# Delta stage: the output gates' projections dealt over the stage and kept in DRAM, the values beside the blockwise inverses

## The chip, the cores and the metric

One core of a Trainium2 chip. The metric is device time in microseconds. The core's engines are named as in the profile: PE is TensorE (PEld its weight loads), DVE is VectorE, ACT is ScalarE, POOL is GpSimd, SP is the engine that issues most DMAs. Each engine runs its own instructions in order and waits for the others on semaphores.

## The reference, cut to what matters

The program is a mixer with a layer of experts, a banded attention and, last, a gated delta rule over 256 tokens and 16 meta tokens (`L` = 272, width 1024). Only the last part, the delta stage, is touched:

```
def deltanet_mixer(h, norm_w, w_in, conv_w, a_log, dt_bias, o_norm_w, w_out):
    u = rms_norm(h, norm_w) @ w_in
    qkv, z, b, a = jnp.split(u, ...)
    qkv = jax.nn.silu(causal_depthwise_conv(qkv, conv_w))
    q, k, v = ...                       # 8 heads of q and k, 16 of v, 128 wide
    o = chunked_gated_delta_rule(q, k, v, beta, g)
    o = rms_norm(o, o_norm_w) * jax.nn.silu(z)
    return o.reshape(B, L, DN_VALUE_WIDTH) @ w_out
...
def step(S, inp):                       # one chunk of the delta rule
    m = strictly_lower(kb @ kc.T * decay)
    sol = triangular_solve(m + eye, rhs)
    u, w = sol[..., :DN_HEAD_DIM_V], sol[..., DN_HEAD_DIM_V:]
    v_new = u - w @ S
    o = (qc * exp(gcum)) @ S + attn @ v_new
    S = S * exp(g_last) + k_state.T @ v_new
```

The gate is `silu(z)`. It is first needed when the outputs `o` are scaled, at the very end; it depends on nothing but the normalised input `h` and 16 blocks of the weights.

## The kernel before

All products are fp32 split in two parts, `hi` and `lo`, and take three matmuls. The work comes in units (`unit`, L269): SP loads a 512 KB block of weights `raw`, ScalarE rounds it to `hi`, VectorE takes the residual `lo` (L274), and TensorE runs 24 matmuls (L284, L285, L286 in turn, the third with `lo`) into a PSUM bank `pj_ps`, of which there are two. The ring of weights has four `raw`, three `hi` and three `lo`. `proj_t` and `proj` are the functions; the delta stage has 49 units: one for the decays (`ba`), 8 for k, 8 for q (260 columns), 16 for v (272 columns), 16 for the gates z (256 columns).

A keys' unit is scaled by the norm's `R` on its way out of PSUM (`cpad`, L1324), since the normalised input isn't there yet; later ones use the normalised `nh`, `nl` and are evicted by ScalarE (`cpad` L1327, `craw` or `qT` L1328). VectorE runs the causal convolution (L1339), four taps each.

Behind the keys come the products `kk`, their norms (`kkd` L1409 and L1410), `lbeta`, sixteen exponentials on ScalarE (L1392, `hh<-dec`), and the matrices `U` (L1483), in two halves. These are stored to DRAM (`e<-U`, L1486) and loaded in another layout (`ab<-e`, L1505), 128 matrices of 32x32, each on one partition. VectorE inverts them by substitution in 31 steps of two operations (`subst`: `sb_t` L1236, `ub` L1238). The result goes through DRAM again (`e<-ub`, `U<-e`), and 8 groups of four heads are put together by small matmuls (`r`, `zt`, `z`, L1533 to L1559): the blockwise inverse.

The substitution and the blockwise inverse are a generator, `inverse()`. The main line is another, `values()`, and whenever it yields, `next(side, None)` issues a piece of the inverse: three steps (`SR` = 3), or a third of a group. The scheduler puts each engine's instructions in its own order, by its own model of their times; `issue_after` pins an instruction behind another.

In the main line stand the 8 units of q, the 16 of v with their norms, transposes and products `attend`, then the gates of heads 0 to 7 (8 units, in `gates`, kept in SBUF as `z`). Then the recurrence runs by groups of four heads (`first(h0)`), where `first(8)` and `first(12)` each run four more gates ahead of their step. The out projection (`w_o`, 16 units of 512 columns) is last.

Of the kernel before, what the change touches and what calls it, by code (L numbers as in the profile page):

```python
# [6 lines left out]
F32 = mybir.dt.float32  # L7
# [10 lines left out]
T = 256  # L18
M = 16
L = M + T  # L20
# [170 lines left out]
class Net:  # L191
    def __init__(self, nc, tc, ap, cat, dat, dump):
        self.nc, self.tc, self.ap, self.dump = nc, tc, ap, dump
        self.cat, self.dat = cat, dat
        self.open = []

    def pool(self, name, bufs=1, space=None, side=None):
        kw = {}
# [69 lines left out]
    def unit(self, src, eng=None):  # L268
        nc = self.nc  # L269
        raw = self.fetch(src)  # L270
        hi = self.ring.tile([128, 1024], F32R, name="hi", bufs=3)
        lo = self.ring.tile([128, 1024], F32R, name="lo", bufs=3)
        nc.scalar.activation(hi, raw, AF.Copy)  # L273
        self.residual = (eng or nc.vector).tensor_sub(lo, raw, hi).ins  # L274
        return hi, lo

    def split(self, hi, lo, src):
# [947 lines left out]
    def subst(self, u, a, n, work, eng):  # L1225

        nc = self.nc
        p = a.shape[0]
        nc.gpsimd.memset(u, 0.0)
        diag = bass.AP(tensor=u.tensor, offset=u.offset, ap=[list(u.ap[0]), [n + 1, n]])  # L1230
        nc.gpsimd.memset(diag, 1.0)
        for s in range(n - 1):
            r = n - 1 - s
            t = work.tile([128, 256], F32, name="sb_t", bufs=1)[:p, :(s + 1) * r]
            t = t.rearrange("p (j c) -> p j c", c=r)
            eng.tensor_tensor(t, u[:, 0:s + 1, s:s + 1].to_broadcast([p, s + 1, r]),  # L1236
                              a[:, s, None, s + 1:].to_broadcast([p, s + 1, r]), op=ALU.mult)
            eng.tensor_sub(u[:, 0:s + 1, s + 1:], u[:, 0:s + 1, s + 1:], t)  # L1238
            yield

    def delta(self, NZ=2, AH=4, KN=8, SS=1, SR=3, SW=3):
        nc, ap = self.nc, self.ap
        ident, tri = self.c("ident"), self.c("tri")
        conv = self.d("conv").rearrange("p (b i) -> p b i", i=4)
# [1 line left out]
        A = self.pool("deA", side="right")  # L1246
# [7 lines left out]
        (hh, hl), R = self.hT, self.R  # L1254
        V = self.pool("deV", side="right")
        W = self.pool("deW1", side="right")
        units = iter(range(49))
        CH = (slice(0, M), slice(M, M + 128), slice(M + 128, L))


# [4 lines left out]
        def normalise(k):  # L1265
            t = W.tile([128, L], F32, name="nt", bufs=2)
            nc.vector.tensor_mul(t, h4[:, k], R)
            self.split_scaled(nh[:, k], nl[:, k], t, gd[:, k:k + 1])

        def proj(ts=slice(0, L)):  # L1270
            ps = pj.tile([128, 512], F32, name="pj_ps", tag="pj")
            n = ts.stop - ts.start
            u = next(units)
            a = (hh, hl) if u <= KN else (nh, nl)
            self.proj_t(ps[:, :n], self.unit(ap["w_t3"][u]), (a[0][:, :, ts], a[1][:, :, ts]))
            return ps[:, :n]


        X = Slices(V.tile([128, 2048], F32, name="early", tag="8"))
        bt = X.tile([128, L], F32, name="bat")  # L1280
        nc.vector.tensor_mul(bt, proj(), R)
        tp = bank(pb, "tp")
        for c in (1, 2, 0):
            nc.tensor.transpose(tp[:CH[c].stop - CH[c].start, c], bt[:, CH[c]], ident)
# [30 lines left out]
        def conv_head(dst, b, t0=0):  # L1315

            n = L - t0
            t = max(t0 - 4, 0)
            w = [conv[:, b, i:i + 1] for i in range(4)]
            ps = proj(slice(t, L))  # L1320
            src = W.tile([128, L], F32, name="cpad", bufs=2)[:, :L - t]
            early = 8 <= b < 8 + KN
            if early:
                nc.vector.tensor_mul(src, ps, R)  # L1324
                ps = src
            else:
                nc.scalar.activation(src, ps, AF.Copy)  # L1327
            nc.scalar.activation(dst, ps[:, t0 - t:t0 - t + n], AF.Copy, scale=w[3])  # L1328
            for i in (2, 1, 0):

                o = max(3 - i - t0, 0)
                at = t0 - t - 3 + i + o
                x, y = src[:, at:at + n - o], dst[:, o:]
                if early and i == 2:
                    x2 = W.tile([128, L], F32, name="ctap", bufs=2)[:, :n - o]
                    nc.scalar.activation(x2, x, AF.Copy, scale=w[i])
                    nc.gpsimd.tensor_add(y, y, x2)
                else:
                    nc.vector.scalar_tensor_tensor(y, x, w[i], y, op0=ALU.mult, op1=ALU.add)  # L1339
# [72 lines left out]
        def norms(c, p):  # L1412
# [6 lines left out]
            if c < 2:  # L1419
                nc.vector.tensor_tensor(bw[:p, c], bw[:p, c], lb[:p, c], op=ALU.add)  # L1420
                nc.scalar.activation(bw[:p, c], bw[:p, c], AF.Exp)

        for j in range(8):
            conv_head(kT[:, j], 8 + j)
            normalise(j)
            if j == 2:
                cumulate()
            if j in (3, 5, 7):
                silu(kT[:, (0 if j == 3 else j - 1):j + 1])
# [74 lines left out]
        def inverse():  # L1504
            nc.sync.dma_start(ab, e1.rearrange("k b m s c -> (k b m) s c"))  # L1505
            ub = V.tile([128, 32, 32], F32, name="ub", tag="4b")
            for s, _ in enumerate(self.subst(ub, ab, 32, V, nc.vector)):
                if s % SR == SR - 1:
                    yield
            nc.sync.dma_start(e2.rearrange("k b m s c -> (k b m) s c"), ub)  # L1510
            for c in range(2):
                for b, s in enumerate(blocks):
# [56 lines left out]
        def values():  # L1569
            for j in range(8):  # L1570
                conv_head(qT[:, j], j, M)
            v.extend(half("v", c) for c in range(2))
            for h0 in range(0, 16, 4):
                hs = slice(h0, h0 + 4)
                raw = A.tile([128, 4, L], F32, name="craw", bufs=2)
                for j in range(4):
                    conv_head(raw[:, j], 16 + h0 + j)
                    if h0 and j % 2:
                        attend(j // 2, h0 - 4)
                    yield  # L1580
                silu(qT[:, h0 // 2:h0 // 2 + 2], silu(raw))
                for c in range(2):
                    tp = bank(pb, "tp")
                    for j in range(4):
                        nc.tensor.transpose(tp[:, j], raw[:, j, CH[c + 1]], ident)
                    for j in range(0, 4, 2):
                        nc.scalar.activation(v[c][:, h0 + j:h0 + j + 2], tp[:, j:j + 2], AF.Copy,
                                             scale=ri[:, c + 1, (h0 + j) // 2:(h0 + j) // 2 + 1])
                tp = bank(pb, "tp")
                for j in range(4):  # L1590
                    nc.tensor.transpose(tp[:M, j], raw[:, j, CH[0]], ident)
                va = W.tile([M, 4, 128], F32, name="va")
                nc.scalar.activation(va, tp[:M], AF.Copy)
                tp = bank(pb, "tp")
                for j in range(2):
                    nc.tensor.transpose(tp[:M, j], kT[:, h0 // 2 + j, CH[0]], ident)
                ka = W.tile([M, 2, 128], F32, name="ka")
                nc.scalar.activation(ka, tp[:M, 0:2], AF.Copy)
                ps = bank(pb, "mv")
                for j in range(4):  # L1600
                    nc.tensor.matmul(ps[:M, j], um[:, h0 + j], va[:, j], start=True, stop=True,
                                     skip_group_check=True)
                vs = W.tile([M, 4, 128], F32, name="vsA")
                nc.vector.tensor_tensor(vs, ps[:M], bw[:M, 0, hs, None].to_broadcast([M, 4, 128]), op=ALU.mult)
                ps = bank(pb, "mS")
                for j in range(2):
                    nc.tensor.matmul(flat(ps[:, 2 * j:2 * j + 2]), ka[:, j],
                                     flat(vs[:, 2 * j:2 * j + 2]), start=True, stop=True, skip_group_check=True)
                nc.scalar.activation(S[:, hs], ps, AF.Copy)
            for c in range(2):  # L1610
                attend(c, 12)
                yield
            for h0 in range(0, 4 * NZ, 4):
                z = A.tile([128, 4, T], F32, name="z", tag="craw", bufs=2)
                yield from gates(z)
                sz.append(z)
            self.logexp()

        def gates(z):
            for j in range(4):  # L1620
                silu(z[:, j], src=proj(slice(M, L)))
                yield

        sz = []
        done = []
        side = inverse()
        for _ in values():
# [2 lines left out]


        W = self.pool("deW3", side="right")
        onw = self.d("onw")


# [77 lines left out]
        def first(h0):  # L1713
            while (int(h0 >= AH), (h0 - AH) % 16) not in done:
                next(side)
            if h0 >= 4 * NZ:
                z = W.tile([128, 4, T], F32, name=f"z{h0}")
                for _ in gates(z):
                    pass
                sz.append(z)  # L1720
            yield from step(0, h0)

        staged((first(h0) for h0 in range(0, 16, 4)), lambda: [next(side, None) for _ in range(SS)])
# [76 lines left out]
```

## Time and profile before

| | |
|---|---|
| median of 3 runs | 1470.29 us (1468.67 to 1470.91) |
| the profiled execution | 1471.06 us, span 1469.3 us |
| delta stage in the span | from about 1165 us to the end |
| TensorE busy, whole span | 1441.3 us |
| VectorE busy, whole span | 1066.4 us |
| ScalarE busy, whole span | 794.1 us |
| mean granted clock of TensorE | 0.997 |

The span is the time from the first to the last instruction of one profiled execution; 1.8 us lie outside it. Busy times come from the page, and the stage's start from the times of its first matmuls. A row of the trace in time has start, length, engine, line and operation, what is written from what, and in brackets how long the engine stood idle before it and what ended that.

### The profile page before, as it was taken

The numbers are of one execution on the slowest core, as the hardware profiler recorded it, in microseconds if no ns is written. First come the engines' busy times: TensorE is split into PE (matmuls) and PEld (weight loads), VectorE is DVE, ScalarE is ACT, GpSimd is POOL, SyncE is SP. The second block draws the span as 40 slices with busy tenths as digits, with TensorE's granted clock in tenths as the row PEclk, the third lists the DMA queues.
The fourth block names the chain that finished last, engine by engine and source line by source line (L and its number), as shares of the span: only waits on it lengthen the run. The fifth ranks groups of instructions, "written<-read, shape, count | busy, mean of one in ns | idle before, by whom it ended". The sixth has DMA issues, their size and how long they took to land.

```text
span 1469.3 us, 27077 instructions
## 1 busy us (share of the span) xinstructions
PE 1441.3 (98%) x10627; PEld 1323.1 (90%) x10627; DVE 1066.4 (73%) x2127; ACT 794.1 (54%) x1367; POOL 73.8 (5%) x106
## 2 busy tenths in 40 slices
PE   9999999999999999999999999999999989999998
PEld 9889999999999999999888888888898989899777
DVE  7667578789948888898555555555776788895566
ACT  5556545545544444444444445444686667664464
POOL 0000000000000000000000000000113024000020
PEclk9999999999999999999999999999999999999999
DMA  7453364555665545545666666666442444545113
GB/s 244 128 163 93 115 207 143 173 172 161 199 179 161 163 150 168 159 155 168 196 189 198 191 195 197 195 192 192 152 117 85 145 120 129 170 124 158 36 43 115
DMA packets 72223, 229.19 MB, mean 156 GB/s; under 512 B 16048, under 2 KB 16464, under 8 KB 72096
## 3 DMA queue, kind: packets, MB, share of 16 engines
q1 hardware_dynamic: 71408, 225.69, 50.5%
q8 instruction: 83, 1.36, 0.4%
q0 software_dynamic: 400, 1.46, 0.3%
q10 hardware_dynamic: 288, 0.33, 0.1%
q14 instruction: 44, 0.36, 0.1%
HBM read 225.31 MB, written 2.13 MB: 155 GB/s over the span
## 4 chain that ended last, share of the span: by engine, by line
PE 93%; ACT 3%; DVE 2%; issue 1%; DMA 0%; SPq 0%; POOL 0%; ACTq 0%; DVEq 0%
PE pu_ps L284 10%; PE pu_ps L285 9%; PE pu_ps L286 9%; PE acc L284 8%; PE acc L285 8%; PE acc L286 8%; PE pj_ps L284 8%; PE pj_ps L285 8%; PE pj_ps L286 8%; PE pt_ps L912 2%; PE tr_ps L370 1%; PE out L284 1%; PE out L285 1%; PE out L286 1%; ACT hi L273 1%
## 5 line engine op out<-in xcount | busy, mean ns | idle before, releaser
L273 ACT ACTIVATE hi<-raw 128x1024 fp32r<-128x1024 f32 x421 | 444.7, 1058 | 433.8 <-PE pu_ps L285 165.8
L274 DVE TENSOR_TENSOR lo<-raw,hi 128x1024 fp32r<-128x1024 f32 x421 | 516.4, 1228 | 197.1 <-ACT hi L273 195.6
L284 PE MATMUL pu_ps<-x2h,hi 128*128 128x256 f32 x1152 | 330.8, 288 | 0.1
L285 PE MATMUL pu_ps<-x2l,hi 128*128 128x256 f32 x1152 | 326.4, 284 | 0.2 <-DVE x2l L279 0.2
L286 PE MATMUL pu_ps<-x2h,lo 128*128 128x256 f32 x1152 | 326.0, 283 | 0.2 <-DVE lo L274 0.2
L285 PEld LDWEIGHTS pu_ps<-x2l,hi 128*128 128x128 f32 x1152 | 220.9, 192 | 0.4 <-DVE x2l L279 0.4
L286 PEld LDWEIGHTS pu_ps<-x2h,lo 128*128 128x128 f32 x1152 | 220.7, 192 | 0.4 <-DVE lo L274 0.4
L284 PEld LDWEIGHTS pu_ps<-x2h,hi 128*128 128x128 f32 x1152 | 220.5, 192 | 0.3 <-ACT x2h L278 0.3
L285 PE MATMUL acc<-lo,ch 128*128 128x512 f32 x512 | 198.8, 389 | 0.0
L286 PE MATMUL acc<-hi,cl 128*128 128x512 f32 x512 | 198.2, 389 | 0.0
L284 PE MATMUL acc<-hi,ch 128*128 128x512 f32 x512 | 139.0, 389 | 0.0
L284 PE MATMUL pj_ps<-hh,hi 128*128 128x272 f32 (+1 forms) x424 | 123.4, 295 | 4.2 <-DVE cpad L1324 2.6
L285 PE MATMUL pj_ps<-hl,hi 128*128 128x272 f32 (+1 forms) x424 | 123.8, 293 | 0.7 <-DVE hl L330 0.6
L286 PE MATMUL pj_ps<-hh,lo 128*128 128x272 f32 (+1 forms) x424 | 123.7, 293 | 0.0
L286 PEld LDWEIGHTS acc<-hi,cl 128*128 128x128 f32 x512 | 96.1, 188 | 20.0
L285 PEld LDWEIGHTS acc<-lo,ch 128*128 128x128 f32 x512 | 96.1, 188 | 19.8
L284 PEld LDWEIGHTS acc<-hi,ch 128*128 128x128 f32 x512 | 96.0, 188 | 19.9
L284 PE MATMUL pj_ps<-nh,hi 128*128 128x256 f32 (+2 forms) x320 | 93.5, 292 | 2.2 <-ACT craw L1328 2.1
L285 PE MATMUL pj_ps<-nl,hi 128*128 128x256 f32 (+2 forms) x320 | 92.8, 290 | 0.0
L286 PE MATMUL pj_ps<-nh,lo 128*128 128x256 f32 (+2 forms) x320 | 92.1, 288 | 0.0
L284 PEld LDWEIGHTS pj_ps<-hh,hi 128*128 128x128 f32 x424 | 80.1, 190 | 5.9 <-issue 2.9
L285 PEld LDWEIGHTS pj_ps<-hl,hi 128*128 128x128 f32 x424 | 80.7, 190 | 2.0 <-DVE hl L330 1.1
(566 smaller groups left out, 2435.5 us busy)
## 6 DMA issues: line engine op xcount, KB each, us to landing
raw<-w_u SPq DMA_DIRECT2D x128, 512.0 KB, 3.7
raw<-w_v SPq DMA_DIRECT2D x128, 512.0 KB, 3.8
raw<-w_t SPq DMA_DIRECT2D x106, 512.0 KB, 3.7
raw<-w_o SPq DMA_DIRECT2D x32, 512.0 KB, 3.6
raw<-w_q SPq DMA_DIRECT2D x16, 512.0 KB, 3.6
raw<-w_br SPq DMA_DIRECT2D x8, 512.0 KB, 3.6
raw<-w_c SPq DMA_DIRECT2D x4, 512.0 KB, 3.7
xT<-xT SPq DMA_DIRECT2D x4, 256.0 KB, 5.1
```

The source lines that it names most:

```text
L273: nc.scalar.activation(hi, raw, AF.Copy)
L274: self.residual = (eng or nc.vector).tensor_sub(lo, raw, hi).ins
L284: mm(out, a[0], b[0], start=start, stop=False, **kw)
L285: mm(out, a[0], b[1], start=False, stop=False, **kw)
L286: mm(out, a[1], b[0], start=False, stop=stop, **kw)
L370: nc.tensor.transpose(tp[:, j], b, self.c("ident"))
L912: nc.tensor.matmul(ps[:, j], at[:, r, j // 2, :, j % 2], bt[:, j // 2, :, j % 2], start=j == 0 and r == 0, stop=r == 1, skip_group_check=True)
```

## The change

The keyword `NZ` and the function `gates` go. A new function `gate(m)` projects gate m, applies silu and stores the result in a DRAM tile `zd` by GpSimd's queue. Gates 0 to 3 run beside keys 4 to 7 (`early`, scaled by `R` on VectorE). Gates 4 to 11 stand behind q and ahead of v; with each, three steps of the substitution are issued, at high priority and pinned behind that gate's residual, and the next unit's residual is pinned behind the last of the three (`pace`). So the 16 units of v now stand beside the blockwise inverse. Gates 12 to 15 are projected in `first(12)`. The twelve stored gates are loaded back when `values()` is done. `proj` gets its unit's number instead of taking the next.

```diff
     def unit(self, src, eng=None):
...
-        self.residual = (eng or nc.vector).tensor_sub(lo, raw, hi).ins
+        with ExitStack() as stack:
+            if self.pace is not None:
+                stack.enter_context(self.tc.issue_after(self.pace))
+                self.pace = None
+            self.residual = (eng or nc.vector).tensor_sub(lo, raw, hi).ins
...
-        def proj(ts=slice(0, L)):
+        def proj(u, ts=slice(0, L), early=False):
...
+        zd = dr.tile([3, 128, 4, T], F32, name="zd")
+
+        def gate(m, early=False):
+            ps = proj(33 + m, slice(M, L), early)
+            st = W.tile([128, T], F32, name="zst", bufs=3)
+            if early:
+                nc.vector.tensor_mul(st, ps, R[:, M:])
+            silu(st, src=st if early else ps)
+            nc.gpsimd.dma_start(zd[m // 4, :, m % 4], st)
+
         for j in range(8):
             conv_head(kT[:, j], 8 + j)
             normalise(j)
+            if j >= 8 - NE:
+                gate(j - 8 + NE, True)
...
             ub = V.tile([128, 32, 32], F32, name="ub", tag="4b")
-            for s, _ in enumerate(self.subst(ub, ab, 32, V, nc.vector)):
-                if s % SR == SR - 1:
-                    yield
+            steps = self.subst(ub, ab, 32, V, nc.vector)
+            next(steps)
+            for n in [SR] * 11:
+
+                with self.tc.high_priority(), self.tc.issue_after(self.residual):
+                    for _ in range(n):
+                        next(steps, None)
+                self.pace = self.sub
+                yield
...
             v.extend(half("v", c) for c in range(2))
+            for m in range(NE, 12):
+                gate(m)
+                yield
             for h0 in range(0, 16, 4):
...
                     yield
+                    if h0 >= 4:
+                        yield
...
-                ka = W.tile([M, 2, 128], F32, name="ka")
+                ka = W.tile([M, 2, 128], F32, name="ka", tag="gt")
...
-            for h0 in range(0, 4 * NZ, 4):
-                z = A.tile([128, 4, T], F32, name="z", tag="craw", bufs=2)
-                yield from gates(z)
-                sz.append(z)
-            self.logexp()
...
+        sz = [A.tile([128, 4, T], F32, name="z", tag="craw", bufs=2) for _ in range(2)]
+        sz += [W.tile([128, 4, T], F32, name=f"z{h0}") for h0 in (8, 12)]
+        for m in range(3):
+            nc.gpsimd.dma_start(sz[m], zd[m])
...
-            if h0 >= 4 * NZ:
-                z = W.tile([128, 4, T], F32, name=f"z{h0}")
-                for _ in gates(z):
-                    pass
-                sz.append(z)
+            if h0 == 12:
+                for j in range(4):
+                    silu(sz[3][:, j], src=proj(45 + j, slice(M, L)))
```

**VectorE, from the last `U` to the substitution.** The rows of the kernel before, behind its last four `U` products (`lo` is a unit's residual, `craw` the convolution of a value unit, `sb_t` the first step):

```order
L1339 SCALAR_TENSOR_TENSOR craw<-cpad,dat_sb,craw 128x271
L1339 SCALAR_TENSOR_TENSOR craw<-cpad,dat_sb,craw 128x270
L274 TENSOR_TENSOR lo<-raw,hi 128x1024
L1339 SCALAR_TENSOR_TENSOR craw<-cpad,dat_sb,craw 128x269
L274 TENSOR_TENSOR lo<-raw,hi 128x1024
L1339 SCALAR_TENSOR_TENSOR craw<-cpad,dat_sb,craw 128x271
L274 TENSOR_TENSOR lo<-raw,hi 128x1024
L1339 SCALAR_TENSOR_TENSOR craw<-cpad,dat_sb,craw 128x270
L1339 SCALAR_TENSOR_TENSOR craw<-cpad,dat_sb,craw 128x271
L1339 SCALAR_TENSOR_TENSOR craw<-cpad,dat_sb,craw 128x269
L1339 SCALAR_TENSOR_TENSOR craw<-cpad,dat_sb,craw 128x270
L1236 TENSOR_TENSOR sb_t<-ub,ab 128x31
```

And of the changed kernel, from the same four products on; its lines are numbered five or six higher (`lo` L279, `sb_t` L1242, `ub` L1244), and `qT` is the convolution of q:

```order
L1501 TENSOR_TENSOR U_13227<-hh_13738,kk 128x512 x4
L1344 SCALAR_TENSOR_TENSOR qT<-cpad,dat_sb,qT 128x256 x6
L1242 TENSOR_TENSOR sb_t<-ub,ab 128x31
L1244 TENSOR_TENSOR ub<-ub,sb_t 128x31
L1242 TENSOR_TENSOR sb_t<-ub,ab 128x60
L1244 TENSOR_TENSOR ub<-ub,sb_t 128x2x30
L1242 TENSOR_TENSOR sb_t<-ub,ab 128x87
L1244 TENSOR_TENSOR ub<-ub,sb_t 128x3x29
L279 TENSOR_TENSOR lo<-raw,hi 128x1024
L1242 TENSOR_TENSOR sb_t<-ub,ab 128x112
L1244 TENSOR_TENSOR ub<-ub,sb_t 128x4x28
L1242 TENSOR_TENSOR sb_t<-ub,ab 128x135
```

Three residuals and eight convolution operations stood ahead of the first step; now none does, and the next residual stands behind three steps. The same pattern, three steps and a residual, repeats behind it. On TensorE, 6 matmuls of q and then value units stood behind the last `kk`; now 65 of q stand there, then 192 of 256 columns, the gates 4 to 11.

**SP, the trip of the second half of `U` through DRAM.** Before (`raw` is a weight block, `um` belongs to the meta tokens):

```order
L1465 DMA um<-d_13627 16x16x16
L265 DMA raw<-w_t 128x1024
L1486 DMA e_13230<-U_13227 32x16x32 x4
L265 DMA raw<-w_t 128x1024
L1505 DMA ab<-e_13230 128x1024
L265 DMA raw<-w_t 128x1024 x21
```

And in the changed kernel:

```order
L1483 DMA um<-d_13768 16x16x16
L266 DMA raw<-w_t 128x1024
L1504 DMA e_13230<-U_13227 32x16x32 x4
L1523 DMA ab<-e_13230 128x1024
L266 DMA raw<-w_t 128x1024 x10
L1534 DMA e_13231<-ub 128x1024
```

The load of `ab` follows the stores with no weight block between them, and ten weight blocks, not twenty-one, stand between `ab` and the store of the result.

**TensorE, the last groups of the blockwise inverse.** Before, part of them, in front of and between the steps of the recurrence (`kS`, `vn`):

```order
L1645 MATMUL kS<-S,kT 128x256 x2
L1541 MATMUL zt<-pr,U_13227 32x32 x4
L1545 MATMUL z_15526<-U_13227,pr 32x32 x8
L1553 MATMUL r_15542<-pr,U_13227 64x64 x4
L1645 MATMUL kS<-S,kT 128x256 x2
L1559 MATMUL z_15549<-U_13227,rn 64x64 x4
```

And in the changed kernel, right ahead of the recurrence (`mv`, `mS`, `kq` are products of the values, `kS` is the recurrence):

```order
L1583 MATMUL z_15729<-U_13227,rn 64x64 x4
L1630 MATMUL mv<-va,um 16x128 x4
L1565 MATMUL zt<-pr,U_13227 32x32 x4
L1569 MATMUL z_15795<-U_13227,pr 32x32 x8
L1577 MATMUL r_15816<-pr,U_13227 64x64 x4
L1636 MATMUL mS<-vsA,ka 128x256 x2
L1515 MATMUL kq<-qT,kT 128x128 x2
L1667 MATMUL kS<-S,kT 128x256 x2
L1583 MATMUL z_15823<-U_13227,rn 64x64 x4
```

The inverse now ends with the values' last products among its links, before the recurrence begins; behind these rows come the 96 matmuls of gates 12 to 15, with the recurrence between them.

## Rows read from the trace of the kernel before

**Rows 1.** Page: busy time, share of the span, instructions of each engine.
```profile
PE 1441.3 (98%) x10627; PEld 1323.1 (90%) x10627; DVE 1066.4 (73%) x2127; ACT 794.1 (54%) x1367; POOL 73.8 (5%) x106
```

**Rows 2.** TensorE's waits, 1160 to 1470 us: total, times, longest.
```profile
PE pj_ps L284 <- DVE cpad L1324: 2.6, 1, 2.6
PE pj_ps L284 <- ACT craw L1328: 2.1, 2, 1.5
PE kk L1399 <- ACT kT L1344: 1.7, 1, 1.7
PE tp L1596 <- ACT v L1587: 1.4, 1, 1.4
...
PE tp L1585 <- ACT craw L1344: 1.1, 1, 1.1
PE r L1553 <- ACT pr L1547: 0.8, 2, 0.6
PE r L1553 <- DVE v L1650: 0.8, 1, 0.8
```

**Rows 3.** Stretches: length, busy us (instructions) by engine, clock, DMA share, GB/s.
```profile
1180.00:1190.00 10.00, 7.43 (x47) 7.24 (x46) 8.98 (x22) 4.68 (x8) 2.53 (x1) 0.83 0.51 157
1252.00:1325.00 73.00, 69.89 (x546) 64.59 (x545) 67.01 (x139) 47.57 (x87) 0.00 (x0) 1.00 0.45 138
1363.00:1404.00 41.00, 38.24 (x443) 32.12 (x443) 23.81 (x72) 19.43 (x40) 3.13 (x5) 1.00 0.07 25
```

**Rows 4.** TensorE in time: start, length, operation, idle before.
```profile
1230.15 0.28 PE L285 MATMUL pj_ps<-nl,hi 128*128 128x260 f32 x1
1230.27 0.28 PE L286 MATMUL pj_ps<-nh,lo 128*128 128x260 f32 x1
...
1232.30 1.11 PE L1399 MATMUL kk<-kT 128*128 128x128 f32 x8
...
1241.87 0.40 PE L284 MATMUL pj_ps<-nh,hi 128*128 128x272 f32 x1 [1.50 <-ACT craw L1328]
```

**Rows 5.** VectorE in time, from `kk` to the first step.
```profile
1236.67 0.19 DVE L1418 TENSOR_TENSOR lbeta<-lbeta,ss 128x16 f32<-128x16 f32 x1
...
1241.18 0.69 DVE L1483 TENSOR_TENSOR U<-hh,kk 128x512 f32<-128x512 f32 x1 [0.35 <-ACT hh L1392]
...
1242.80 1.22 DVE L274 TENSOR_TENSOR lo<-raw,hi 128x1024 fp32r<-128x1024 f32 x1
1243.94 0.50 DVE L1339 SCALAR_TENSOR_TENSOR craw<-cpad,dat_sb,craw 128x269 f32<-128x269 f32 x1
...
1252.05 0.19 DVE L1236 TENSOR_TENSOR sb_t<-ub,ab 128x31 f32<-128x31 f32 x1 [3.04 <-DMA ab<-e]
```

**Rows 6.** ScalarE's groups, 1165 to 1404 us: busy us, mean ns.
```profile
L1392 ACT ACTIVATE hh<-dec,lbeta 128x128 f32<-128x128 f32 x16 | 4.2, 418 | 0.7 <-DVE lbeta L1418 0.7
...
L1344 ACT ACT_TABLE_LOAD x2 | 2.6, 1283 | 1.0 <-DVE craw L1339 1.0
```

**Rows 7.** SP's queue in time.
```profile
1241.90 3.52 SPq L1486 DMA_DIRECT2D e<-U  x4
...
1246.90 0.34 SPq L1505 DMA_DIRECT2D ab<-e  x1
```

**Rows 8.** VectorE in time, one step of the substitution.
```profile
1314.03 0.37 DVE L1236 TENSOR_TENSOR sb_t<-ub,ab 128x207 f32<-128x207 f32 x1
1314.44 0.37 DVE L1238 TENSOR_TENSOR ub<-ub,sb_t 128x207 f32<-128x207 f32 x1
```

**Rows 9.** VectorE's groups, 1252 to 1326 us.
```profile
L1236 DVE TENSOR_TENSOR sb_t<-ub,ab 128x31 f32<-128x31 f32 (+15 forms) x31 | 10.4, 336 | 3.4 <-DMA ab<-e 3.0
L1238 DVE TENSOR_TENSOR ub<-ub,sb_t 128x31 f32<-128x31 f32 (+15 forms) x31 | 10.4, 335 | 0.2
```

**Rows 10.** GpSimd in time, and a DMA of its queue.
```profile
1184.41 2.53 POOL L1337 TENSOR_TENSOR kT<-kT,ctap 128x271 f32<-128x271 f32 x1 [5.72 <-ACT ctap L1336]
...
sk<-w_sk POOLq DMA_DIRECT2D x2, 512.0 KB, 6.1
```

More of the change, by code (lines that the diff above doesn't have):

```diff
@@ L1 @@
 import math
+from contextlib import ExitStack
 import numpy as np
@@ L194, in __init__ @@
         self.cat, self.dat = cat, dat
-        self.open = []
+        self.open, self.pace = [], None
     def pool(self, name, bufs=1, space=None, side=None):
@@ L1237, in subst, with delta @@
                               a[:, s, None, s + 1:].to_broadcast([p, s + 1, r]), op=ALU.mult)
-            eng.tensor_sub(u[:, 0:s + 1, s + 1:], u[:, 0:s + 1, s + 1:], t)
+            self.sub = eng.tensor_sub(u[:, 0:s + 1, s + 1:], u[:, 0:s + 1, s + 1:], t).ins
             yield
-    def delta(self, NZ=2, AH=4, KN=8, SS=1, SR=3, SW=3):
+    def delta(self, AH=4, NE=4, SS=1, SR=3, SW=3):
         nc, ap = self.nc, self.ap
@@ L1256, in delta @@
         W = self.pool("deW1", side="right")
-        units = iter(range(49))
         CH = (slice(0, M), slice(M, M + 128), slice(M + 128, L))
@@ L1268, in normalise @@
             self.split_scaled(nh[:, k], nl[:, k], t, gd[:, k:k + 1])
-        def proj(ts=slice(0, L)):
+        def proj(u, ts=slice(0, L), early=False):
             ps = pj.tile([128, 512], F32, name="pj_ps", tag="pj")
             n = ts.stop - ts.start
-            u = next(units)
-            a = (hh, hl) if u <= KN else (nh, nl)
+            a = (hh, hl) if early else (nh, nl)
             self.proj_t(ps[:, :n], self.unit(ap["w_t3"][u]), (a[0][:, :, ts], a[1][:, :, ts]))
@@ L1280, in delta @@
         bt = X.tile([128, L], F32, name="bat")
-        nc.vector.tensor_mul(bt, proj(), R)
+        nc.vector.tensor_mul(bt, proj(0, early=True), R)
         tp = bank(pb, "tp")
@@ L1319, in conv_head @@
             w = [conv[:, b, i:i + 1] for i in range(4)]
-            ps = proj(slice(t, L))
+            early = 8 <= b < 16
+            ps = proj(b - 7 if early else b + 9 if b < 8 else b + 1, slice(t, L), early)
             src = W.tile([128, L], F32, name="cpad", bufs=2)[:, :L - t]
-            early = 8 <= b < 8 + KN
             if early:
@@ L1580, in values @@
                     yield
+                    if h0 >= 4:
+                        yield
                 silu(qT[:, h0 // 2:h0 // 2 + 2], silu(raw))
@@ L1612, in values @@
                 yield
-            for h0 in range(0, 4 * NZ, 4):
-                z = A.tile([128, 4, T], F32, name="z", tag="craw", bufs=2)
-                yield from gates(z)
-                sz.append(z)
-            self.logexp()
[L1619 to L1624, printed above, removed]
         done = []
```

## The prediction

> **What bounds the kernel now.** I read the page first. TensorE is busy for 98% of the span [rows 1], so a change that keeps the same matmuls can win only what TensorE still waits, and can lose wherever it makes TensorE wait. The changed program has the same matmuls; only their places differ. So I went on to the list of what TensorE waits for from 1160 us to the end, which is the delta stage [rows 2]. The reader is to see there that no wait repeats: 2.6 us on a key's `cpad` product, 1.7 us ahead of `kk`, 2.1 us (two times) and 1.1 us on ScalarE's `craw` work, 1.4 us on `v`, and two rows of short waits of the blockwise inverse, `r`. Then the table of stretches [rows 3]: between 1180 and 1190 us the granted clock is 0.83, because the 2.6 us wait was followed by matmuls at the lower level (1.2 GHz); 0.17 of 10 us is another 1.7 us. From 1252 to 1325 us, where the substitution runs now, VectorE is busy 67.01 of 73 us and TensorE 69.89: the two are nearly level there. All of it together is some 14 us, the most that better covering could win.
>
> Last I followed the one long dependence that the change touches, from the last `kk` matmul to the first substitution step. It starts at 1233.4 us, where `kk` ends [rows 4]. On VectorE come the reduction, `lbeta` at 1236.67, and four `U` products, the last ending at 1241.87 [rows 5]; they wait on ScalarE's sixteen exponentials, which take 4.2 us [rows 6]. Then SP issues four stores of `U` (3.52 us), and at 1246.90 the load of `ab` [rows 7], which lands for the first step at 1252.05. So the chain takes 18.6 us, of which 10.2 us lie behind the last `U`, where only transfers run. In this kernel TensorE doesn't feel that: VectorE stands still for just 3.04 us ahead of the step [rows 5], since in its order (printed in the section on the change) three residuals `lo` and eight `craw` operations stand between `U` and the step, and those residuals keep TensorE in work.
>
> **The change, step by step.** *The new wait.* In the changed order VectorE has one residual, that of gate 4, behind the last `kk` reduction, and then the first three substitution steps; the residual of gate 5 stands behind these. VectorE runs in order, so while it waits for `ab`, no weight block can be made ready. I take the chain at its measured 18.6 us: of its parts, VectorE's list up to `U` is nearly the same, ScalarE's exponentials are the same, and of SP's only the weight load between the stores and `ab` is gone (`ab` could start 0 to 1 us earlier, since it waits for the stores to land as well). The first three steps are 31, 60 and 87 elements wide and cost .2 to .25 us an operation, with .04 us between two (0.37 long, .41 apart [rows 8]): 1.5 us. The residual takes 1.2 us. So TensorE gets gate 5's third matmul 18.6 + 1.5 + 1.2 = 21.3 us after `kk`. What does it have until then? By the order 65 matmuls of q (260 columns, .12 us apart [rows 4]) are 7.8 us, gate 4's 24 are 2.9 us, two matmuls of gate 5 that need no residual .2 us: 10.9 us. It stands idle for 21.3 - 10.9 = **10.4 us**, in one piece or with about 1 us of it ahead of gate 4, whose PSUM bank ScalarE frees only behind the exponentials. Bounds: 5 us, if stores, load and exponentials run without today's neighbours, and 13 us if they meet more.
>
> *The substitution beside the gates.* From there on VectorE has, for each gate, three steps and a residual. A step pair in the middle is two operations of .37 us, .41 apart [rows 8], so three are 2.46 us; all 62 sum to 20.8 us [rows 9], which with .04 each gives 2.25 us for an average three, ends included. The residual costs 1.14 us from start to start [rows 5]. That is 3.6 us for a gate against TensorE's 24 x .12 = 2.86. Seven such rounds lie between gate 5's residual and that of the first value block: 7 x 3.6 = 25.2 against 20.0 us, **+5.2 us** (3.7 with the average). Before, the same steps lay beside 16 value units and cost little: the three waits of 1252 to 1325 us, which are removed below.
>
> *The clock.* After the long wait I expect the lower level again, as behind the 2.6 us wait, which cost 1.7 us [rows 2, 3]. Here the price is hidden at first: TensorE has about .75 us of slack in each of the next rounds, so 1.7 us are made good in three of them. I take 0, bound 1.7.
>
> *Early gates 0 to 3.* Each adds a product of 256 columns (at most the .50 us of a 269-column `craw` operation [rows 5]) and a residual (1.14 us) to VectorE beside 2.9 us of TensorE, and so gives VectorE room. The 2.6 us wait stands behind the fifth key, for the PSUM bank of the fourth, with VectorE busy 8.98 of 10 us there [rows 3]; gate 0 now comes at that place and needs the same bank, so the wait stays, with its clock. The 1.7 us ahead of `kk` should go: two more units stand in between. **-1.7.** Two more loads of an activation table, 1.28 us each [rows 6], fall on ScalarE, which has room there (4.68 us busy of 10 [rows 3]): 0, at most 2.6 if that room is gone.
>
> *Values beside the inverses.* The two `craw` waits (2.1), `craw` L1344 (1.1) and `v` (1.4) belong to places that no longer exist: **-4.6**. In their place each value unit (24 matmuls of 272 columns, 3.0 us by the .12 us of 260) has a residual, four convolution operations and a share of the inverse's copies; VectorE's sum stays below TensorE's, so only hiccups of latency remain, put at **+2** (0 to 6, by the 4.6 just named). The round trip of the finished substitution through DRAM lies beside three value units and costs nothing; without them it would be another chain of transfers like that above.
>
> *Recurrence.* The rows `r` of the inverse sum to 1.6 us [rows 2]. Its last two groups still run with no projection between, ahead of gates 12 to 15; I leave 1.0: **-0.6** (-1.6 to +3).
>
> *Gates through DRAM.* Twelve stores and three loads on GpSimd's queue, far apart from their use; 0 if three `zst` buffers suffice.
>
> Sum: 10.4 + 5.2 + 2 - 1.7 - 4.6 - 0.6 = **+10.7 us**. The profiled execution took 1471.06 us, so 1481.8; the median is .77 lower, so **1481 us**.
>
> **A page against the row.** The windows of the recurrence and inverse show many short waits and a granted clock of 1.00 [rows 3], so short waits cost no clock there. The Trainium skill, "TensorE: Matmul & The Clock Gate", section "A second HAM failure mode: psum-queue depth-cycling", says that frequent micro-idles between groups of matmuls can make the clock swing between its two levels. By that rule the gates' seven short waits could keep the clock low, and the sum would be the third rival's, 1496; by the rows it stays at 1481.
>
> **Rivals.** *Faster: the chain is much shorter than today.* If `U`, stores and load take 13 us, not 18.6 + 1.5 + 1.2, because what stands between them today is gone, TensorE idles 2 us; beside the gates it loses 3.7; with 2 of hiccups, less the 6.9 removed, the sum is +0.8. Were the 2.6 us wait and its 1.7 us of clock gone too, since the key stage has more cover, it is 1470.3 + 0.8 - 4.3 = 1467. It decides for a gain below some 2 us of idling. Against it: 3.52 us of issuing, then the stores' landing, and 5.1 us of loading behind 1246.90 alone are 10.2 us, and they don't overlap.
>
> *No change:* the chain comes to the 5 us bound of idling, the rounds to 3.7 and the value stretch to no hiccup: 5 + 3.7 - 6.9 = +1.8, 1472. It needs three bounds at once.
>
> *Slower than forecast: the clock stays low in the gates.* At half clock a gate takes twice 2.86 us, 2.1 more than its round: 7 x 2.1 = 15, so 1496. For it: after 1183 us the low clock did follow a wait. Against it: the clock of the recurrence.
>
> *Slower: the stores of the gates.* A GpSimd add takes up to 2.53 us beside VectorE's work, and a load issued by GpSimd lands after up to 6.1 us [rows 10]. If stores are held by the substitution, `zst` runs out behind three gates, and the PSUM banks with it: a gate would then cost 6.1 us less the 3.6 us round, 2.5; for the five gates behind the third it is 12, so 1493. In a sentence beside it: the Trainium skill, "SBUF — State Buffer", section "SBUF: two separate sides", says that a DMA from GpSimd's queue needs its descriptors written through a port pair that VectorE can hold, which speaks for this rival; no row here shows a store held so.
>
> **Chances.** Forecast (1476 to 1486) 0.52, low clock or held stores (1487 to 1497) 0.14, small losses below 1476 0.04, no change 0.12, faster 0.18. What this kernel's measurement can tell from no change is about 0.2%, 2.9 us: slower 0.70, same 0.12, faster 0.18. The range for 8 in 10 is 1466 to 1490 us, from the faster rival's value to where the slow rivals begin to bite; the forecast's own is 1476 to 1486.
>
> **What would show it.** In the changed profile I expect one TensorE wait of 8 to 11 us in gate 5, on its residual `lo`, VectorE idle on the DMA of `ab` for about as long, granted clock near half behind it, and VectorE near 100% through the gates while TensorE waits about .75 us a gate on `lo`. The value stretch should show TensorE above 95%, and no wait on GpSimd or on `zst`. I am wrong if VectorE doesn't idle ahead of the first step, if TensorE's wait there is below 5 us, or if the value stretch loses more than 6 us.

## The result, and the profile after

The change makes the kernel slower: 1478.64 us median (1478.22 to 1479.45, 6 runs) against 1469.81 us (1468.02 to 1471.38, 6 runs), a ratio of 1.0059 (1.005 to 1.0069), 8.8 us. The profiled execution took 1478.22 us with a span of 1476.4, 7.1 us over the span before, which was one of the longer runs of its kernel. In the page, VectorE's share of the chain that ended last is 3%, where it was 2%:

```profile
PE 92%; DVE 3%; ACT 2%; issue 1%; DMA 0%; POOL 0%; SPq 0%; ACTq 0%; DVEq 0%
```

The list of TensorE's waits from 1160 us to the end (total, times, longest), the answer to [rows 2]:

```profile
PE pj_ps L291 <- DVE lo L279: 5.4, 5, 3.9
PE pj_ps L289 <- ACT zst L1349: 3.6, 2, 2.5
PE pj_ps L289 <- DVE cpad L1329: 2.6, 1, 2.6
PE dS L1698 <- ACT k L1695: 1.6, 1, 1.6
PE pj_ps L289 <- ACT qT L1333: 1.4, 1, 1.4
PE out L289 <- ACT o1at L283: 1.3, 1, 1.3
...
PE r L1577 <- ACT pr L1571: 0.3, 1, 0.3
```

The `kk`, `craw` and `v` waits of [rows 2] are gone, 6.3 us together. The 2.6 us on `cpad` stand as before. New are 5.4 us on the residual `lo`, 3.6 us on `zst`, and 1.6 us on `k` in the recurrence. The 1.4 us wait on ScalarE's `qT` stands at the place of the longer `craw` wait of [rows 4], behind the exponentials.

Where the new waits lie is seen on TensorE in time (start, length, operation, idle before), the answer to [rows 4]:

```profile
1234.08 1.11 PE L1404 MATMUL kk<-kT 128*128 128x128 f32 x8
...
1244.79 0.39 PE L289 MATMUL pj_ps<-nh,hi 128*128 128x256 f32 x1 [1.40 <-ACT qT L1333]
...
1250.62 0.39 PE L289 MATMUL pj_ps<-nh,hi 128*128 128x256 f32 x1 [2.48 <-ACT zst L1349]
...
1255.01 0.58 PE L291 MATMUL pj_ps<-nh,lo 128*128 128x256 f32 x1 [3.89 <-DVE lo L279]
```

Gate 4 starts 1.40 us late, since its bank waits for the exponentials. At 1250.62 the first matmuls of gate 6, which the order puts ahead of gate 5's third, wait for gate 4's bank (ScalarE loads an activation table before that gate's silu); they only fill a part of the longer wait. At 1255.01 gate 5's third matmul waits for its residual. These three make 7.77 us of idling, with one gate between them. VectorE's list says why, the answer to [rows 5]:

```profile
1238.45 1.22 DVE L279 TENSOR_TENSOR lo<-raw,hi 128x1024 fp32r<-128x1024 f32 x1 [1.29 <-ACT hi L274]
...
1244.13 0.69 DVE L1501 TENSOR_TENSOR U<-hh,kk 128x512 f32<-128x512 f32 x1 [0.34 <-ACT hh L1397]
...
1252.33 0.19 DVE L1242 TENSOR_TENSOR sb_t<-ub,ab 128x31 f32<-128x31 f32 x1 [3.50 <-DMA ab<-e]
...
1253.74 1.22 DVE L279 TENSOR_TENSOR lo<-raw,hi 128x1024 fp32r<-128x1024 f32 x1
...
1256.75 1.22 DVE L279 TENSOR_TENSOR lo<-raw,hi 128x1024 fp32r<-128x1024 f32 x1
...
1278.36 1.22 DVE L279 TENSOR_TENSOR lo<-raw,hi 128x1024 fp32r<-128x1024 f32 x1
```

The first step waits 3.50 us for `ab`, and the next residual, that of gate 5 at 1253.74, stands behind three steps. Between two residuals the rounds then take 3.0 us, and up to 3.8 in the middle. The residual at 1278.36 is that of the first value block: the seven rounds take 24.6 us. On SP ([rows 7]):

```profile
1244.84 2.11 SPq L1504 DMA_DIRECT2D e<-U  x4
1248.81 0.34 SPq L1523 DMA_DIRECT2D ab<-e  x1
```

Stores and load are quicker than before: 2.11 us of issuing against 3.52, and 3.5 us from the load's issue to the first step against 5.15. SP issues no weight block from 1244 to 1255 us; before, one stood between the stores and `ab`, and more followed right behind it. From the end of `U` to the step it is 7.5 us, where it was 10.2. Stretches (length, busy us by engine from TensorE on, granted clock third from the end):

```profile
1252.00:1256.00 4.00, 0.99 (x4) 0.99 (x5) 3.40 (x11) 0.00 (x0) 0.00 (x0) 0.55 0.09 33
1256.00:1260.00 4.00, 4.00 (x24) 4.00 (x23) 3.76 (x10) 0.26 (x1) 0.00 (x0) 0.59 0.64 179
1260.00:1264.00 4.00, 4.00 (x37) 4.00 (x35) 3.83 (x9) 2.40 (x4) 0.57 (x2) 1.00 0.58 155
1290.00:1340.00 50.00, 50.00 (x521) 44.69 (x520) 40.74 (x81) 33.53 (x67) 0.79 (x4) 1.00 0.48 146
```

Behind the wait the granted clock is near the lower level until about 1260 us; 1256 to 1260 alone loses 1.6 us, and the microsecond ahead of it some 0.4. From 1290 to 1340 us, where the values stand beside the inverses, TensorE never stops.

### The profile page after: what moved, and what is told of

Read it like the earlier page. It is cut to its first block, busy times and chain, and to the rows that moved or that the text cites. A ratio compares the mean times of both kernels' runs of the same rounds, so it can differ in the third digit from the quotient of the medians.

```text
span 1476.4 us, 27117 instructions
## 1 busy us (share of the span) xinstructions
PE 1443.9 (98%) x10627; PEld 1325.0 (90%) x10627; DVE 1072.3 (73%) x2131; ACT 796.7 (54%) x1368; POOL 82.1 (6%) x121
## 4 chain that ended last, share of the span: by engine, by line
PE 92%; DVE 3%; ACT 2%; issue 1%; DMA 0%; POOL 0%; SPq 0%; ACTq 0%; DVEq 0%
PE pu_ps L289 9%; PE pu_ps L290 9%; PE pu_ps L291 9%; PE acc L289 8%; PE acc L290 8%; PE acc L291 8%; PE pj_ps L289 7%; PE pj_ps L291 7%; PE pj_ps L290 7%; PE pt_ps L917 2%; DVE lo L279 1%; PE out L289 1%; PE tr_ps L375 1%; PE out L290 1%; PE out L291 1%
## 5 line engine op out<-in xcount | busy, mean ns | idle before, releaser
L279 DVE TENSOR_TENSOR lo<-raw,hi 128x1024 fp32r<-128x1024 f32 x421 | 516.4, 1228 | 197.2 <-ACT hi L274 195.7
L289 PE MATMUL pj_ps<-hh,hi 128*128 128x256 f32 (+1 forms) x456 | 132.4, 294 | 4.3 <-DVE cpad L1329 2.6
L290 PE MATMUL pj_ps<-hl,hi 128*128 128x256 f32 (+1 forms) x456 | 132.7, 292 | 0.7 <-DVE hl L335 0.6
L291 PE MATMUL pj_ps<-hh,lo 128*128 128x256 f32 (+1 forms) x456 | 132.6, 292 | 0.0
L289 PEld LDWEIGHTS acc<-hi,ch 128*128 128x128 f32 x512 | 96.1, 188 | 19.8
L289 PEld LDWEIGHTS pj_ps<-hh,hi 128*128 128x128 f32 x456 | 86.2, 190 | 6.1 <-issue 3.0
L291 PE MATMUL pj_ps<-nh,lo 128*128 128x272 f32 (+2 forms) x288 | 85.2, 296 | 5.4 <-DVE lo L279 5.4
L289 PE MATMUL pj_ps<-nh,hi 128*128 128x272 f32 (+2 forms) x288 | 84.8, 294 | 5.0 <-ACT zst L1349 3.6
L290 PEld LDWEIGHTS pj_ps<-hl,hi 128*128 128x128 f32 x456 | 86.7, 190 | 2.0 <-DVE hl L335 1.1
L291 PEld LDWEIGHTS pj_ps<-hh,lo 128*128 128x128 f32 x456 | 86.6, 190 | 1.4 <-issue 0.7
```

Source lines behind the costliest of these rows:

```text
L289: mm(out, a[0], b[0], start=start, stop=False, **kw)
L290: mm(out, a[0], b[1], start=False, stop=False, **kw)
L291: mm(out, a[1], b[0], start=False, stop=stop, **kw)
```

## The experiments

My theory: the loss is the wait for `ab` with the next gate's residual queued behind it, and VectorE's rounds of three steps and a residual behind that. Rivals: the gates' stores on GpSimd's queue; the new places of gates and values themselves. Ratios are to the kernel before, run beside each experiment, where the change itself has 1.0059.

**Two more residuals ahead of the first step.** In `inverse()`, ahead of the loop over the steps:

```diff
+            for _ in range(2):
+                yield
             for n in [SR] * 11:
```

> Two more gates' residuals stand ahead of the first substitution step; nothing else is moved. If the loss is the wait for the load of the matrices with the next residual queued behind it, TensorE has three gates (8.6 us) instead of one (2.9 us) to run in that time: of the 7.8 us of idling some 2 to 3 stay, the 1.9 us of low clock behind it goes, and the time falls by 6 to 7 us, to about 1472 (2 us over the kernel before). If the loss lies in the gates' way through DRAM, or in the values beside the inverses, it stays where it is, 8 to 9 us over the kernel before.

Measured: 1475.13 us, 1.0039 (1.0026 to 1.0053): a gain of some 3 us, half of what was expected. TensorE's waits, and stretches:

```profile
PE pj_ps L291 <- DVE lo L279: 6.3, 7, 1.8
...
PE pj_ps L289 <- ACT qT L1333: 1.4, 1, 1.4
...
PE pj_ps L289 <- ACT zst L1349: 1.1, 1, 1.1
```

```profile
1255.69 0.38 PE L291 MATMUL pj_ps<-nh,lo 128*128 128x256 f32 x1 [1.72 <-DVE lo L279]
...
1281.87 0.39 PE L291 MATMUL pj_ps<-nh,lo 128*128 128x272 f32 x1 [1.76 <-DVE lo L279]
```

```profile
1250.00:1260.00 10.00, 8.29 (x68) 7.89 (x67) 6.65 (x19) 4.54 (x8) 1.67 (x3) 1.00 0.67 213
1260.00:1270.00 10.00, 8.62 (x69) 7.99 (x68) 9.55 (x20) 3.99 (x6) 1.62 (x3) 1.00 0.56 188
...
1370.00:1374.00 4.00, 4.00 (x17) 3.52 (x16) 1.85 (x5) 0.63 (x1) 0.00 (x0) 0.50 0.01 2
```

The mechanism is there: the wait for `ab` is 1.4 + 1.7 us (at 1255.69) where it was 7.8, and the clock stays at 1.00 behind it. But the rounds now cost 4.6 + 1.1 = 5.6 us of waits, where the changed kernel shows 2.6. Of these, 2.4 us stand at gates, where no low clock hides any of them now. The other 3.2 us, three waits from 1281 to 1290 us, stand at value units (272 columns): the substitution starts two units later, so its last rounds lie beside those, which give VectorE three convolution operations each on top of the steps. And the clock falls at another place, to 0.50 at 1370 us, in the last groups of the inverse.

**One residual fewer.** A `yield` ahead of the loop over the gates, so that gate 4's residual also stands behind the first three steps.

> The first three steps are pinned one unit earlier, behind the residual of the last unit of q, so that gate 4's residual too stands behind the wait. By the same theory TensorE has 2.9 us less to run: 11.5 us over the kernel before (10 to 13). By the others nothing changes: 8 to 9 us over.

Measured: 1478.31 us, 1.006 (1.0044 to 1.0075): no change against the changed kernel. By the time alone that is what the rivals had said, and not the 10 to 13 us of my theory; the rows decide. Its waits, and its first step:

```profile
PE pj_ps L291 <- DVE lo L279: 6.8, 2, 6.4
PE pj_ps L289 <- ACT qT L1333: 2.8, 2, 1.7
```

```profile
1250.28 0.19 DVE L1242 TENSOR_TENSOR sb_t<-ub,ab 128x31 f32<-128x31 f32 x1 [2.73 <-DMA ab<-e]
```

The wait did grow, to 6.4 + 2.8 = 9.2 us, by 1.5 and not 2.9. The step comes 16.9 us after the start of the last `kk` (1233.42 us), where it was 18.3 (1234.08 to 1252.33): in the changed kernel gate 4's residual stands ahead of `lbeta`, in the chain itself, and waits there 1.29 us for ScalarE's `hi`. The rounds then lose 1.2 us less. So a residual ahead of the step is cover for TensorE and a length of the chain at once; the expectation counted the first alone.

**The scheduler's own order.** No pin, no priority; gates and values at their new places:

```diff
-                with self.tc.high_priority(), self.tc.issue_after(self.residual):
-                    for _ in range(n):
-                        next(steps, None)
-                self.pace = self.sub
+                for _ in range(n):
+                    next(steps, None)
```

> The steps are not pinned to the residuals and have no priority; gates and values stay at the new places. The scheduler's order has three more residuals ahead of the first step. By the theory of the wait the idling goes but for 1 to 2 us: within 2 us of the kernel before. By the theory that the places of gates and values cost the time: 8 to 9 us over.

Measured: 1473.83 us (1468.85 to 1475.91), 1.0021 (1.0012 to 1.003): better than the change, but 3 to 4 us over the kernel before and not within 2. No row of `lo` or `zst` is left in its list of waits, so the pins and not the places made them: the rival of the places falls for this stretch. Its stretches:

```profile
1250.00:1260.00 10.00, 10.00 (x86) 10.00 (x86) 7.76 (x20) 5.28 (x8) 2.21 (x4) 1.00 0.92 307
...
1332.00:1336.00 4.00, 2.94 (x59) 2.10 (x57) 3.86 (x10) 2.28 (x6) 0.00 (x0) 1.00 1.01 243
1336.00:1340.00 4.00, 3.44 (x27) 2.43 (x26) 2.38 (x7) 1.46 (x4) 0.20 (x1) 0.52 0.70 213
1340.00:1344.00 4.00, 4.00 (x42) 3.59 (x42) 2.06 (x5) 0.71 (x3) 0.00 (x0) 0.50 0.01 2
1344.00:1348.00 4.00, 4.00 (x35) 2.83 (x35) 1.21 (x4) 2.85 (x9) 0.20 (x1) 0.50 0.01 4
```

From 1250 to 1260 us TensorE is busy throughout at clock 1.00. But in the inverse the clock falls: behind a stretch in which TensorE is busy 2.94 of 4 us, it is at 0.52 from 1336 us, and it stays at 0.50 to 1348 while TensorE is busy 4.00 of 4 us. There run the small matmuls of the inverse (32x32 and 64x64) and of the values, with no projection between. The eleven runs go from 1468.85 us at a mean clock of 0.993 to 1475.91 at 0.987.

**Two steps for each unit.** `for n in [2] * 16` for `[SR] * 11`.

> Two steps for each unit instead of three, pinned in the same way. A round on VectorE is then two steps (1.64 us) and a residual (1.14), 2.8 us, level with TensorE's 2.86: the 2.6 us of waits in the rounds go, and the first wait is .5 us shorter; the substitution ends five units later, which may leave blocks of the inverse without cover at the end (0 to 3 us). Time 4 to 8 us over the kernel before. If VectorE in the rounds is not what binds, no gain: 9 us over or more.

Measured: 1471.72 us, 1.0014 (1.0005 to 1.0023): 2 us over the kernel before, less than the 4 to 8 that were expected. The row of the waits on `lo`, and all that is left behind 1363 us:

```profile
PE pj_ps L291 <- DVE lo L279: 4.4, 3, 3.0
...
PE out L289 <- ACT o1at L283: 1.2, 1, 1.2
...
PE vn L1677 <- DVE v L1672: 0.6, 1, 0.6
PE z L1583 <- ACT rn L1580: 0.5, 1, 0.5
```

3.0 us of it are the first wait, which with `zst` and `qT` still makes 6.9 us; between 1256 and 1287 us no wait is left. VectorE's rounds were a cost of their own. But they are only part of the 7 us: `lo`, `zst` and `qT` together fell by 2.1 us, and the waits behind 1363 us by 2.6 (from 4.9 to 2.3), the 1.6 us on `k` among them. The inverse ends later here, its last link at 1397.74 us between the steps of the recurrence (1375.93 in the changed kernel); that its links fill those waits is how I read it, not tested by itself.

**Both.** Two residuals ahead and two steps for each unit.

> Two more residuals ahead of the first step, and two steps for each unit instead of three. If the wait for the load and VectorE's rounds are two separate costs, both go: 4.7 us of idling and 1.9 us of low clock by the first, and the rounds' 5.6 us (as they show without the low clock) by the second; against that, the substitution ends some ten units later, and the last groups of the inverse may stand without projections: up to 5 us. Time between 4 us under and 3 us over the kernel before. If both had one cause, it is no better than two steps alone (2 us over).

Measured: 1470.27 us, 1.0006 (0.9994 to 1.0018): the gains add up nearly, to the kernel before. One wait of 2.9 us is left at the first step:

```profile
PE pj_ps L291 <- DVE lo L279: 4.4, 4, 2.9
```

**Three residuals ahead, two steps.** As above with `range(3)`.

> Three more residuals ahead of the first step (before: two), two steps for each unit. The run with two ahead still waited 2.9 us for the residual behind the load; one more gate is 2.9 us of work, so that wait goes but for half a microsecond. Time 2 to 3 us under that run, 1 to 2 us under the kernel before, if the inverse, which ends another unit later, doesn't lose its cover and the clock; if it does, no gain.

Measured: **1465.30 us** (1464.05 to 1467.48), 0.9958 (0.9945 to 0.9972): 5 us faster than the kernel before and 13 faster than the change. The longest of its waits:

```profile
PE pj_ps L289 <- DVE cpad L1329: 2.6, 1, 2.6
PE pj_ps L289 <- ACT craw L1333: 1.4, 1, 1.4
PE pj_ps L289 <- ACT qT L1333: 1.4, 1, 1.4
PE out L289 <- ACT o1at L283: 1.2, 1, 1.2
```

None is on `lo` or `zst`. The change's own gains stay: no `kk` wait, and the inverses under the values. It gained twice what was expected: against the run with two ahead all 4.4 us on `lo` went, not 2.9 alone. Its nine executions show a mean clock of 0.995 to 0.998.

**The early gates alone.** Gates 4 to 11 go back behind the values and the substitution beside them, unpinned.

> Of the change only gates 0 to 3 beside the keys and the way of the gates through DRAM are kept; gates 4 to 11 go back behind the values, and the substitution runs beside the values without a pin, as before. If early gates and stores cost nothing and take the 1.7 us wait ahead of kk away, the time is 1 to 2 us under the kernel before. If the stores, or the loads of activation tables, cost time, it is over it by what they cost. TensorE should wait for no zst and no GpSimd DMA.

Measured: 1470.54 us (1463.34 to 1473.61), 0.9996 (0.9981 to 1.001): inconclusive by its times, since they follow the clock: 1463.34 us at a mean clock of 0.999, 1473.61 at 0.989. In the profiled one the clock is at the lower level for some 25 us in the inverse, as in this stretch:

```profile
1364.00:1370.00 6.00, 5.45 (x61) 4.33 (x60) 2.93 (x10) 1.19 (x4) 0.20 (x1) 0.50 0.00 0
```

The `kk` wait is gone and no wait on `zst` appears. At a like clock this run is the faster one: 1465.31 and 1465.69 us at 0.997, where the kernel before, run beside it, took 1468.94 to 1470.62 at 0.997. That is some 4 us, nearly all of the 5 us that the fastest run above gains over its own kernel before; what that run adds is a clock that hardly falls (0.995 to 0.998, here 0.989 to 0.999). **Gates 8 to 11 back in the recurrence as well** was to bring the clock back:

```diff
-            for m in range(NE, 12):
+            for m in range(NE, 8):
...
-            if h0 == 12:
+            if h0 >= 8:
```

> As the run with the early gates alone, but gates 8 to 11 go back to the recurrence, where the kernel before has them; so the kernel before with gates 0 to 3 moved beside the keys, and nothing else. In the run with the early gates alone the clock was low for some 25 us while the inverse's small matmuls ran without a projection between them, and its times followed the mean clock (1463.3 us at 0.999, 1473.6 at 0.989). If the missing projections caused that, the clock stays high here in nearly all runs and the time is 3 to 6 us under the kernel before. If it is something else about the early gates, the times scatter as they did, around 1470.

Measured: 1475.63 us (1469.90 to 1477.51), 1.0027 (1.0012 to 1.0043), with clocks from 0.996 to 0.989: a miss. The missing gates 8 to 11 are not what lowers the clock. Here 8 of 12 executions have a mean clock of 0.991 or less, of the kernel before, run beside it, none of 23 (the lowest is 0.992): moving gates 0 to 3 alone makes the fall more frequent. Why is open.

**Early gates behind keys 1 to 4**, in the changed kernel:

```diff
-            if j >= 8 - NE:
-                gate(j - 8 + NE, True)
+            if 1 <= j < 1 + NE:
+                gate(j - 1, True)
```

> The four early gates stand behind keys 1 to 4 instead of 4 to 7, so that VectorE, which falls behind in the key stage, gets its room before the wait on cpad (2.6 us, with 1.5 us of low clock behind it). If VectorE's arrears make that wait, it goes, with its clock, and the time falls by some 4 us against the changed kernel (to 4 to 5 us over the kernel before); the four keys behind may bring up to 2 us of it back ahead of kk. If the wait has another cause (GpSimd's adds, say), nothing changes: 8 to 9 us over.

Measured: 1480.87 us, 1.0082 (1.0069 to 1.0096), slower.

```profile
PE pj_ps L291 <- DVE lo L279: 6.5, 3, 5.5
PE pj_ps L289 <- ACT zst L1349: 3.2, 2, 2.1
PE pj_ps L289 <- ACT qT L1333: 2.6, 2, 1.8
...
PE pj_ps L289 <- DVE cpad L1329: 0.5, 1, 0.5
```

The `cpad` wait fell from 2.6 to 0.5 us, so VectorE's arrears do make it. But TensorE, with that time won, has run gate 4 too by 1244.9 us and only reaches the wait for `ab` sooner, which ends no earlier: 5.5 + 2.1 + 1.8 = 9.4 us. What is saved ahead of a chain that TensorE doesn't set is waited for at its end. **With two residuals ahead and two steps** it was worse than without the move:

> Early gates behind keys 1 to 4, two residuals ahead of the first step, and two steps for each unit. If the three costs are separate, the gains add up: 3 to 4 us under the run with two residuals ahead and two steps, so 2 to 6 us under the kernel before. If it is not faster than that run, the wait in the key stage is not the place of gates 0 to 3.

Measured: 1477.42 us, 1.0059 (1.0046 to 1.0072), 7 us over the run named Both. On SP a weight block stands between the stores and the load of `ab`, which is issued only at 1253.82 us (1247.04 in that run); the first step comes at 1258.84, and TensorE waits 5.4 us in one piece on `lo`. So it does not tell whether the costs are separate. **And behind keys 2 to 5, on the kernel with only the early gates moved** (the run with gates 8 to 11 back is "the run above"):

> As the run above, with the early gates behind keys 2 to 5. VectorE gets its room one to two keys sooner, so that the 2.6 us wait on cpad and its 1.5 us of low clock should go; the last two keys then stand without a gate, and the chain to the substitution starts up to 2 us later, which the values cover here. 0 to 4 us under the run above. If the wait comes back at another key, no change.

Measured: 1470.72 us (1467.83 to 1477.23), 1.0014 (1.0001 to 1.0027): the `cpad` wait is gone here too; the times scatter with the clock (0.999 to 0.989). The median is 4.9 us under that run, but at a like clock nothing is gained: 1470.69 us at 0.996 against 1469.90, 1477.23 at 0.989 against 1476.35 to 1477.51. In its list new waits stand in place of the old one, 1.8 us on the load of `U` and 1.6 on `craw` among them.

**Stores from ScalarE's queue.** `nc.scalar.dma_start` for the twelve stores.

> The changed kernel with the twelve stores of gates issued by ScalarE's queue in place of GpSimd's. If stores are held on GpSimd and hold back zst and TensorE, the time falls by some us against the changed kernel; by the theory of the wait and VectorE's rounds nothing changes: 8 to 9 us over the kernel before, or up to 1 us more for the issuing on ScalarE.

Measured: 1480.43 us, 1.0065 (1.0048 to 1.0083), the same within the interval. In the changed kernel the stores land in 2.8 us (DMA issues, median to landing), and GpSimd waits for silu ahead of each:

```profile
zd<-zst POOLq DMA_DIRECT2D x12, 128.0 KB, 2.8
```

The rival of held stores falls. The Trainium skill's rule on descriptors written through a port that VectorE can hold ("SBUF — State Buffer", section "SBUF: two separate sides") thus cost nothing that these runs show, with VectorE 3.83 of 4 us busy beside the stores at 1260 us.

## Why the prediction was right, step by step

The forecast was 10.7 us on the profiled execution, in which 7.1 was measured; by the medians it was 1481 us for 1478.64, 8.8 us over. The mechanism, a wait at gate 5 behind `ab` and rounds bound by VectorE, is the one that the profile shows and that the pin, the residuals ahead and the steps for each unit move one by one. Nearly every term was put too high, the first above all. Of the signs, two failed by the letter: I had expected one wait of 8 to 11 us on `lo`, and VectorE idle for about as long. It came in three pieces (1.40, 2.48 and 3.89 us), of which the one on `lo` is below the 5 us that I had set as a sign of being wrong, and VectorE idled 3.50 us, since it had six convolution operations of q to run as well. The terms:

- *The new wait:* 10.4 us forecast, 7.8 measured. The chain from the end of `kk` to the step was 17.1 us, not 18.6: 2.7 us were won in stores and load, which meet fewer weight loads, and 1.1 us lost ahead of `U`, where gate 4's residual stands in the chain and waits 1.29 us for `hi` (in the kernel before a unit's residual stood there too, and waited 0.28). I had put stores and load at "0 to 1 us" less and "VectorE's list up to `U`" at nearly the same; these were the slips. TensorE also had about 1.1 us more to run than I counted, two matmuls of gate 6 among it.
- *The rounds and the clock:* 5.2 and 0 forecast. VectorE's seven rounds took 24.6 us, where 25.2 was forecast. Measured on TensorE are 2.6 us of waits and 2.0 us of low clock, 4.6 together, since the slow matmuls run in VectorE's time, as foreseen.
- *Early gates:* -1.7 for the `kk` wait, and the `cpad` wait kept with its clock: both as forecast. The table loads cost nothing there; one lies in the wait at gate 5.
- *Values beside the inverses:* -4.6 came true, the +2 of hiccups did not come: 0 from 1290 to 1340 us. (VectorE has three convolution operations for a value unit, not the four that I counted; the first tap is ScalarE's.)
- *Recurrence:* -0.6 forecast. The inverse's `r` fell to 0.3 us from 1.6, but the recurrence itself waits 1.6 us on `k`, which I had not counted; as I read it, for want of the inverse's links between its steps (with two steps for each unit they stand there, and the wait is gone). From 1363 us on, the waits total .4 us more than before.

With 7.8 + 4.6 - 6.3 + 0.4 the rows give 6.5 of the 7.1 us; the rest stays without a name. Of the rivals, a clock that stays low through the gates did not happen: it was back at 1.00 from 1260 us, and with eight waits of .3 to 1.8 us from 1254 to 1290 us (two residuals ahead) it is 1.00 throughout. The rule that I had set against the rows (the Trainium skill, "TensorE: Matmul & The Clock Gate", section "A second HAM failure mode: psum-queue depth-cycling") is not borne out in that stretch. The *faster* rival asked for 13 us from the end of `kk` to the waiting gate's third matmul; it was 19.8 us here (1235.19 to 1255.01), and 18.4 in the shortest that I read, with no residual ahead of the step.

## What to carry to other kernels

Where a load's result is wanted by an engine that works in order, count what the other engines need from that engine behind the waiting instruction; two or three of its feeding operations ahead of it are worth more than an early start (13 us here between one and four of them, with the steps thinned to the other engine's pace; 2.6 us of that lie in the recurrence). Each thing put ahead tends to lengthen the chain: from the end of `kk` to the first step it was 15.8 us with no residual ahead, 17.1 with one, 17.8 and 19.6 with three, 18.4 with four. So try the number out. Time saved ahead of a chain that the busiest engine doesn't set comes back as a wait at its end.

## What the runs showed of the hardware that was not expected

The same wait does not always cost the clock. In the changed kernel the 2.64 us on `cpad` are followed by a clock of 0.54 and 0.61 (1184 to 1186 and 1186 to 1188 us), and in the kernel before by 0.63 and 0.52; in the run with the early gates alone, the same wait, 2.57 us, is followed by 1.00 in both stretches. So the 1.7 us that I read behind it in [rows 3] are no fixed price of such a wait.

The clock also falls where TensorE hardly waits. In the unpinned kernel it is back at 1.00 from 1350 to 1352 us, then at 0.81 and from 1354 us at 0.50, with TensorE busy 2.00 us in each of these stretches of 2 us, in small matmuls of the inverse and the values with no projection between. It falls in some executions of a kernel and not in others (0.999 to 0.989 in the early gates alone, 1463.3 to 1473.6 us), and some runs of the kernel before show it too (1475.1 us at 0.992). Putting four gates back into the recurrence did not hold it up. What would, stays open.
